# Where a tuned backbone kernel keeps its modulation blocks, and what its first transfers wait for

## The chip, the cores and the metric

One NeuronCore of a Trainium2 chip runs the whole program; the other cores are idle. The metric is the device time of one execution in microseconds, the median over several executions. The engines are named as in the profile: PE is TensorE (matmuls), PEld its weight loads, DVE is VectorE, ACT is ScalarE, POOL is GpSimd and SP is SyncE, whose queue issues nearly all DMAs here.

## The reference

Two layers of a backbone with 1024 features work on 512 latent tokens and 256 context tokens, which share the weights. Each layer has six modulation vectors for the latent tokens and six for the context tokens, made from two conditioning vectors by one large weight matrix per layer:

```python
silu_c, silu_cc = silu(c), silu(c_ctx)
for l in range(DEPTH):
    mod_lat = split(silu_c @ ada_w[l] + ada_b[l], 6)      # ada_w[l]: 1024 x 6144
    mod_ctx = split(silu_cc @ ada_w[l] + ada_b[l], 6)
    z = modulate(x, norm1_w[l], mod[0], mod[1]) @ w_in[l]  # shift, scale
    x = x + mod[2] * merge(hgrn(z), attention(z), conv(z)) @ w_out[l]
    x = x + mod[5] * square(relu(modulate(x, norm2_w[l], mod[3], mod[4]) @ w1[l])) @ w2[l]
```

`modulate` is an RMS norm times `1 + scale` plus shift. The context tokens go through the same steps in layer 0; in layer 1 only their projections are needed, so only shift and scale of the first norm are made for them there. All is float32, with inputs scaled so that low precision would show.

So the modulation is a product of two rows (latent and context) with two matrices of 6.3 million numbers: little arithmetic and much traffic.

## The kernel before

**Large products.** Activations lie with features on partitions. Every float32 product is made of three float32r matmuls: weights and activations are split into a high part and the rest (`wh`, `wl`, `Hh`, `Hl`), and `wh*Hh`, `wh*Hl`, `wl*Hh` are summed in PSUM (`fm`, L224; `tm_in`, L247, gives tokens on partitions). Weights come as **slabs** of 128 x 1024 numbers (512 KB) in a fixed plan of 304. For each slab SP issues a DMA into one of three buffers of the tag `raw` (`dma_slab`, L179), ACT makes `wh` by a copy (L205), DVE makes `wl` by a subtraction (L206). `next_w` (L209) hands out slab n, has slab n+1 split and slabs up to n+3 fetched. PE spends 24 matmuls of 512 columns on a slab for the latent tokens and 24 of 256 columns for the context tokens.

**Modulation, streamed.** `ada_stream` (L352) is a generator: `next_w` calls it once for most slabs, and each call is a step. For each piece (a block of 128 x 1024 numbers of `ada_w`) a step issues the DMA into a buffer of the same tag `raw` (L361, L363), in four strips of 256 columns, that is rows of 1 KB. One step later DVE multiplies the block by the conditioning columns and accumulates (`ada`, L376; L385 and L387): eight operations of 128 x 256 when both token kinds are needed, four when only the latent row is. After every second block follow a transpose, a reduction, eight tiny matmuls (L405) and an addition of the bias (L408). Layer 0's vectors 2, 4, 3, 5 are made in this way during the convolutions and the gates of layer 0 (32 blocks), all of layer 1's during the MLP of layer 0 (48 blocks; vectors 1 and 0 first, for which both rows are needed, 16 blocks). `self.stream` is set in `mlp` (L1117) when the first four slabs of its first quarter are through.

**The MLP.** `mlp` has four quarters e = 0 to 3; each has eight slabs of w1, whose result ACT and DVE square and split (`square`, L1105: L1112 ACT, L1113 DVE, L1114 ACT, L1115 DVE), and eight slabs of w2, whose result DVE adds to x (L1027). In the last quarter of layer 0 the w2 slabs go through `last_products` (L1080), which also gathers the squares for the next norm and begins the next layer's norm.

**The start.** `consts` (L101) issues `cc`, then the eight tiles of x in turn on ACT's and SP's queue, then small constants and the identity, from which DVE makes `sel` (L121). `start` (L299) first fetches two slabs, then block 0 of `ada_w` for the first two vectors (`ada_block`, L270: two transfers of 512 KB each, with rows of 512 bytes, into a ring of six slots; PE multiplies them with 32-column matmuls, L282). `norm_sq` (L433) squares x tile by tile on ACT (L439, L442) and sums on DVE (L443); `norm_rms` (L445) sums over partitions on PE (L452), makes the inverse root in a chain of small DVE operations and a diagonal matrix from it and the identity (L458); `norm_bc` (L462) spreads it on PE (L466). `ada_block_sum` (L286) finishes a block: ACT copy (L290), PE (L292), two DVE operations (L294, L296). Then a loop over k = 0 to 7 fetches block k+3, finishes block k+2, normalizes feature tile k (`norm_apply`, L472: L481 DVE, L483 ACT, L484 DVE) and runs the 18 matmuls of the first projection on it (L338). Its second half (L263) follows.

**The order of the work.** The code is written against a framework whose planner orders each engine's instructions: it runs the program in a model of its own and takes, of what is ready, the instruction of highest priority (earlier in the code is higher; `high_priority(offset=-30)` puts the streamed blocks' DVE work 30 places later). Buffers with a tag are handed out in turn, and whoever wants one waits for its last readers. On the chip each engine, and SP's queue, then takes its instructions in this fixed order.

## Time and profile before

| what | time |
|---|---|
| median of 3 runs | 2505.33 us (2498.78 to 2507.31) |
| profiled execution | 2507.57 us |
| its span, first to last instruction | 2505.8 us |
| PE busy | 2459.6 us (98%) |
| PEld busy | 2111.3 us (84%) |
| DVE busy | 1475.4 us (59%) |
| ACT busy | 812.6 us (32%) |
| POOL busy | 28.0 us (1%) |
| granted TensorE clock, mean | 0.998 |
| read from HBM | 226.49 MB, 92 GB/s over the span |

How to read it: busy time is the union of an engine's instructions. An idle engine costs nothing unless the one that sets the end waits for it. The list of waits puts idle time down to what ended it. A row of the windows gives, for a stretch, the busy time of PE, PEld, DVE, ACT and POOL with the number of instructions, the granted clock, the busy share of the 16 DMA engines and the GB/s. A row of the timeline has start, duration, engine, line, operation, tiles (out<-in) and, in square brackets, the engine's idle time before it with what ended it. Some matmul records can be missing.

### The profile page before, as it was taken

What the parts mean: (1) busy time and instruction counts of PE and PEld (TensorE: products, weight loads), DVE (VectorE), ACT (ScalarE), POOL (GpSimd) and SP (SyncE); (2) the same over time, 40 slices, a digit from 0 to 9 for tenths busy, and PEclk for the clock granted to TensorE, in tenths of its full rate; (3) what the DMA queues carried; (4) which work ended last, traced back from release to release, by engine and by line L of the source; (5) the groups of instructions that cost most, each with busy time, mean ns of one, the idle gap of its engine ahead of it and who ended that gap; (6) DMA issues with size and microseconds to landing.
All of it is one profiled execution on the core that took longest, in us unless ns stands there. A gap on an engine that the chain in (4) does not pass through costs nothing.

```text
span 2505.8 us, 40660 instructions
## 1 busy us (share of the span) xinstructions
PE 2459.6 (98%) x17040; PEld 2111.3 (84%) x17040; DVE 1475.4 (59%) x2952; ACT 812.6 (32%) x1435; POOL 28.0 (1%) x52
## 2 busy tenths in 40 slices
PE   7999999999999999999999999999999999999999
PEld 6888988888888888878888888888878888888887
DVE  6477867776664666675655464787653335634433
ACT  4334365321212233121222333445442223422322
POOL 0000000000000000000000000000000000000000
PEclk9999999999999999999999999999999999999999
DMA  8111112233334212333343222111222233222322
GB/s 267 60 44 45 51 53 69 77 118 118 93 118 143 76 60 85 116 113 125 120 132 119 93 76 74 52 61 49 66 74 97 97 126 108 77 94 93 101 93 93
DMA packets 112344, 233.32 MB, mean 93 GB/s; under 512 B 8224, under 2 KB 65824, under 8 KB 112160
## 3 DMA queue, kind: packets, MB, share of 16 engines
q1 hardware_dynamic: 111584, 229.14, 28.1%
q8 instruction: 134, 2.20, 0.4%
q10 hardware_dynamic: 576, 1.57, 0.2%
q14 instruction: 50, 0.41, 0.1%
HBM read 226.49 MB, written 4.19 MB: 92 GB/s over the span
## 4 chain that ended last, share of the span: by engine, by line
PE 86%; DVE 7%; DMA 5%; ACT 2%; issue 1%; SPq 0%; DVEq 0%; ACTq 0%
PE pl L239 55%; PE pc L239 15%; PE tp L263 4%; DMA ada<-in_ada_w 4%; PE pc L263 2%; DVE adac L387 2%; DVE wl L206 1%; PE av L853 1%; PE ho L645 1%; PE sc L888 1%; PE kvp L621 1%; PE ptp L934 1%; PE lv L551 1%; DVE S L590 1%; PE tp L338 1%
## 5 line engine op out<-in xcount | busy, mean ns | idle before, releaser
L205 ACT ACTIVATE wh<-raw 128x1024 fp32r<-128x1024 f32 x297 | 314.5, 1059 | 849.7 <-PE pl L239 379.2
L239 PE MATMUL pl<-Hh,wh 128*128 128x512 f32 (+1 forms) x1488 | 586.5, 394 | 0.5 <-DVE S L1002 0.5
L239 PE MATMUL pl<-Hh,wl 128*128 128x512 f32 (+1 forms) x1488 | 581.4, 391 | 3.9 <-DVE wl L206 3.9
L239 PE MATMUL pl<-Hl,wh 128*128 128x512 f32 (+1 forms) x1488 | 581.1, 391 | 0.0
L206 DVE TENSOR_TENSOR wl<-raw,wh 128x1024 fp32r<-128x1024 f32 x297 | 363.2, 1223 | 318.5 <-ACT wh L205 313.7
L239 PE MATMUL pl<-S,wh 128*128 128x512 f32 x1392 | 436.4, 395 | 2.9 <-ACT S L1114 2.8
L239 PEld LDWEIGHTS pl<-Hh,wl 128*128 128x128 f32 x1488 | 279.7, 188 | 67.8 <-DVE wl L206 7.0
L239 PEld LDWEIGHTS pl<-Hh,wh 128*128 128x128 f32 x1488 | 279.7, 188 | 57.0 <-issue 0.8
L239 PEld LDWEIGHTS pl<-Hl,wh 128*128 128x128 f32 x1488 | 279.8, 188 | 55.1 <-issue 0.5
L239 PEld LDWEIGHTS pl<-S,wh 128*128 128x128 f32 x1392 | 258.3, 188 | 57.8 <-ACT S L1114 3.2
L239 PE MATMUL pl<-S,wl 128*128 128x512 f32 x696 | 273.8, 393 | 0.0
L387 DVE SCALAR_TENSOR_TENSOR adac<-ada,sc,adac 128x256 f32<-128x256 f32 x448 | 196.4, 481 | 119.4 <-DMA ada<-in_ada_w 116.6
L239 PE MATMUL pc<-Hh,wh 128*128 128x256 f32 x872 | 244.2, 280 | 0.8 <-ACT wh L205 0.6
L239 PE MATMUL pc<-Hh,wl 128*128 128x256 f32 x872 | 244.2, 280 | 0.2 <-DVE wl L206 0.2
L239 PE MATMUL pc<-Hl,wh 128*128 128x256 f32 x872 | 244.2, 280 | 0.0
L239 PEld LDWEIGHTS pc<-Hh,wh 128*128 128x128 f32 x872 | 164.5, 189 | 5.8 <-ACT wh L205 0.8
L239 PEld LDWEIGHTS pc<-Hl,wh 128*128 128x128 f32 x872 | 164.6, 189 | 4.4 <-DVE Hl L484 0.2
L1027 DVE SCALAR_TENSOR_TENSOR S<-pl,mod,S 128x512 f32<-128x512 f32 (+1 forms) x80 | 59.2, 740 | 180.2 <-PE pl L239 180.1
L239 PEld LDWEIGHTS pc<-Hh,wl 128*128 128x128 f32 x872 | 164.3, 188 | 1.0 <-issue 0.4
L239 PEld LDWEIGHTS pl<-S,wl 128*128 128x128 f32 x696 | 131.0, 188 | 30.4
L239 PE MATMUL pc<-S,wh 128*128 128x256 f32 x688 | 127.1, 285 | 0.0
L239 PEld LDWEIGHTS pc<-S,wh 128*128 128x128 f32 x688 | 111.5, 192 | 4.4
(269 smaller groups left out, 3131.7 us busy)
## 6 DMA issues: line engine op xcount, KB each, us to landing
raw<-in_w SPq DMA_DIRECT2D x304, 512.0 KB, 3.3
ada<-in_ada_w SPq DMA_DIRECT2D x80, 512.0 KB, 4.1
S<-in_ada_w SPq DMA_DIRECT2D x16, 512.0 KB, 7.3
B<-in_bias SPq DMA_DIRECT2D x16, 448.0 KB, 4.0
S<-in_xT SPq DMA_DIRECT2D x12, 384.0 KB, 6.0
xs<-S SPq DMA_DIRECT2D x8, 256.0 KB, 2.0
S<-xs SPq DMA_DIRECT2D x8, 256.0 KB, 4.6
out<-S SPq DMA_DIRECT2D x8, 256.0 KB, 2.0
```

Source lines behind the costliest of these rows:

```text
L205: self.nc.scalar.activation(hi, r, AF.Copy)
L206: self.nc.vector.tensor_tensor(lo, r, hi, op=ALU.subtract)
L239: nc.tensor.matmul(p, lhsT=W[:, s], rhs=X[:, t0:t0 + n], start=k == 0 and i == 0, stop=k == nk - 1 and i == 2)
L263: nc.tensor.matmul(o[t], lhsT=X[:, t * 128:t * 128 + 128], rhs=W[:, k4 * 256:k4 * 256 + 256], start=piece == 0 and k4 == 0 and i == 0, sto ...
L338: nc.tensor.matmul(o[t], lhsT=X[:, t * 128:t * 128 + 128], rhs=W[:, c], start=k == 0 and i == 0, stop=k == 7 and i == 2)
L387: nc.vector.scalar_tensor_tensor(out=acc[:, row, :], in0=w, scalar=s, in1=acc[:, row, :], op0=ALU.mult, op1=ALU.add)
L551: nc.tensor.matmul(p[32 * i:32 * i + 32, c * 32:c * 32 + 32], lhsT=lhs(o), rhs=rhs(o), start=True, stop=True, tile_position=(0, 32 * i))
L590: nc.vector.tensor_tensor(qv, qv, tv, op=ALU.mult)
L621: nc.tensor.matmul(kvp[:, i * P:(i + 1) * P], lhsT=kt[:, slots[qd, c]], rhs=vh(c), start=True, stop=True)
L645: nc.tensor.matmul(po[:, i * P:(i + 1) * P], lhsT=lh, rhs=rh, start=n == 0, stop=n == len(mms) - 1)
L853: nc.tensor.matmul(po[64 * pr:64 * pr + 64, o:o + m], lhsT=nv[:, t * 256 + d0:t * 256 + d0 + 64], rhs=pts[pr][:, pc:pc + m], start=n == 0, ...
L1027: nc.vector.scalar_tensor_tensor(out=x, in0=p[:, :n], scalar=self.mod[l][:, m, j, r:r + 1], in1=x, op0=ALU.mult, op1=ALU.add)
```

## The change

Six edits:

1. The streamed blocks get buffers of their own, three of the tag `adaw`, in place of those of `raw`.
2. A block is used two steps after its DMA is issued instead of one, and its sum is finished one step later too; the generator has `len(todo) + 4` steps instead of 3 more.
3. Both kinds of modulation blocks lie in DRAM as they are wanted in SBUF: `ada1` for the start, `ada2` for the stream. A transfer has 128 rows of 4 KB, in place of rows of 512 bytes (start) or 1 KB (stream). The bytes are the same.
4. In the w1 slabs of the quarters e = 0 and e = 1 of the MLP only odd slabs make a step of the stream.
5. The identity is issued right after `cc`, ahead of x; `sel` is made after the squares of x in the code. The first two slabs are issued behind block 1 of the start instead of ahead of block 0, so their splits move behind the sums of the norm too.
6. The diagonal matrix of the start is made in two operations, 256 columns for the context tokens first, then 512.

Beside that, the memory set aside for DMA descriptors made by software is cut to 1024 (no DMA here uses it).

```diff
 consts:
         nc.sync.dma_start(out=cc, in_=self.a["cc"])
+        self.ident = self.cst("ident", [P, P])
         self.X = (11, 12, 13, 2)
...
         self.nw = self.cst("nw", [P, 2, DEPTH, 8])
-        self.ident = self.cst("ident", [P, P])
-        self.sel = sb.tile([P, 32], F32, name="sel")
-        nc.vector.tensor_reduce(out=self.sel, in_=self.ident[:, :].rearrange("p (g i) -> p i g", g=4), op=ALU.add,
-                                axis=mybir.AxisListType.X)
 ada_block:
-            self.new(ring[0])
-            r = self.S[ring[0]][:, 0:1024].rearrange("p (k f) -> p k f", k=8)
-            ring.append(ring.pop(0))
-            f0 = m * D + j * P
-            nc.sync.dma_start(out=r, in_=self.a["ada_w"][0, :, f0:f0 + P].rearrange("(k p) f -> p k f", p=P))
+            slot = ring.pop(0)
+            ring.append(slot)
+            self.new(slot)
+            r = self.S[slot][:, 0:1024].rearrange("p (k f) -> p k f", k=8)
+            nc.sync.dma_start(out=self.S[slot][:, 0:1024], in_=self.a["ada1"][j, 1 - m])
 start:
-        self.dma_slab()
-        self.dma_slab()
         ring = [0, 1, 8, 9, 10, 6]
         mp = {0: self.ada_block(0, ring)}
         self.norm_begin()
         for j in range(8):
             self.norm_sq(j, 0, T)
-        dg = self.norm_rms(0, T)
+        self.sel = self.sb.tile([P, 32], F32, name="sel")
+        nc.vector.tensor_reduce(out=self.sel, in_=self.ident[:, :].rearrange("p (g i) -> p i g", g=4), op=ALU.add,
+                                axis=mybir.AxisListType.X)
+        dg = self.norm_rms(0, T, ((512, 256), (0, 512)))
         mp[1] = self.ada_block(1, ring)
+        self.dma_slab()
+        self.dma_slab()
         self.ada_block_sum(0, mp[0])
 ada_stream:
-        for i in range(len(todo) + 3):
-            if i > 2 and todo[i - 3][2] == 1:
-                self.ada_sum(l, *todo[i - 3][:2], ahead.pop(i - 3))
+        for i in range(len(todo) + 4):
+            if i > 3 and todo[i - 4][2] == 1:
+                self.ada_sum(l, *todo[i - 4][:2], ahead.pop(i - 4))
             if i < len(todo):
                 m, c, kg = todo[i]
-                r = self.raw(f"ada{l}_{m}_{c}_{kg}")
-                f0 = m * D + c * 256
-                self.nc.sync.dma_start(
-                    out=r[:, :].rearrange("p (k f) -> p k f", k=4),
-                    in_=self.a["ada_w"][l, kg * 512:(kg + 1) * 512, f0:f0 + 256].rearrange("(k p) f -> p k f", p=P))
+                r = self.sb.tile([P, 1024], F32, tag="adaw", bufs=3, name=f"ada{l}_{m}_{c}_{kg}")
+                self.nc.sync.dma_start(out=r, in_=self.a["ada2"][l, m, c, kg])
                 ahead[i] = r
-            if 0 < i <= len(todo):
-                m, c, kg = todo[i - 1]
+            if 1 < i <= len(todo) + 1:
+                m, c, kg = todo[i - 2]
                 with self.tc.high_priority(offset=-30):
-                    ahead[i - 1] = self.ada(l, m, kg, ahead.pop(i - 1))
+                    ahead[i - 2] = self.ada(l, m, kg, ahead.pop(i - 2))
             yield
 norm_rms:
-        nc.vector.tensor_tensor(dg.rearrange("p (t q) -> p t q", q=P), self.ident[:, :].unsqueeze(1).broadcast_to([P, nt, P]),
-                                y.unsqueeze(2).broadcast_to([P, nt, P]), op=ALU.mult)
+        for p0, pn in parts or ((0, n),):
+            d = dg[:, p0:p0 + pn].rearrange("p (t q) -> p t q", q=P)
+            nb = [P, pn // P, P]
+            nc.vector.tensor_tensor(d, self.ident[:, :].unsqueeze(1).broadcast_to(nb),
+                                    y[:, p0 // P:(p0 + pn) // P].unsqueeze(2).broadcast_to(nb), op=ALU.mult)
 mlp:
             for f in range(f0, 8):
-                self.square(ff, f, self.fm(self.next_w("mlp_w1", l), *X))
+                self.square(ff, f, self.fm(self.next_w("mlp_w1", l, e > 1 or f % 2 == 1), *X))
 _host:
-    a["ada_w"] = g["ada_w"]
+    a["ada1"] = np.stack([g["ada_w"][0][:, m * D:(m + 1) * D].reshape(8, P, 8, P).transpose(2, 1, 0, 3).reshape(8, P, D)
+                          for m in (1, 0)], 1)
+    a["ada2"] = g["ada_w"].reshape(DEPTH, 2, 4, P, 6, 4, 256).transpose(0, 4, 5, 1, 3, 2, 6).reshape(DEPTH, 6, 4, 2, P, D)
 kernel:
-    nc = _bacc.Bacc("TRN2", target_bir_lowering=False, num_devices=1)
+    nc = _bacc.Bacc("TRN2", target_bir_lowering=False, num_devices=1, dynamic_dma_scratch_size=1024)
```

## The prediction

> **What bounds the kernel now.** I read the page's busy times and its chain first, then the table of waits, then windows cut at the stages, and last the timeline of two places.

> ```profile
> span 2505.8 us, 40660 instructions
> PE 2459.6 (98%) x17040; PEld 2111.3 (84%) x17040; DVE 1475.4 (59%) x2952; ACT 812.6 (32%) x1435; POOL 28.0 (1%) x52
> PE 86%; DVE 7%; DMA 5%; ACT 2%; issue 1%; SPq 0%; DVEq 0%; ACTq 0%
> ```

> TensorE sets the time: 2459.6 of 2505.8 us, so 46.2 us are idle in all. The change touches no big matmul; it can only win idle PE time and time in which PE runs slowly. So the question is where PE stands still because of modulation blocks. The waits:

> ```profile
> DVE adac L387 <- DMA ada<-in_ada_w: 116.6, 37, 5.7
> DVE adac L385 <- DMA ada<-in_ada_w: 84.5, 37, 5.2
> PE adap L282 <- DMA S<-in_ada_w: 16.7, 2, 16.1
> ```

> The columns are total us, times, longest. DVE waits 201 us for streamed blocks, but that is no loss by itself: PE pays only where something behind the waiting DVE instruction is needed at once. The MLP of layer 0 shows where. I cut it at the first matmul that reads Hh (w1 begins) or S (w2 begins); the rows below are w2 of e=0, then w1 and w2 of e=1, w1 and w2 of e=2, w1 and w2 of e=3:

> ```profile
> 991.59:1060.05 68.46, 68.46 (x424) 59.98 (x416) 47.34 (x106) 9.17 (x11) 0.00 (x0) 1.00 0.35 108
> 1060.05:1133.66 73.61, 69.74 (x424) 58.76 (x416) 51.56 (x110) 19.84 (x35) 0.00 (x0) 1.00 0.36 115
> 1133.66:1208.46 74.80, 71.93 (x424) 62.10 (x416) 40.31 (x77) 10.78 (x14) 0.00 (x0) 0.95 0.41 127
> 1208.46:1275.75 67.29, 67.29 (x425) 58.78 (x417) 40.68 (x82) 21.54 (x37) 0.00 (x0) 1.00 0.40 126
> 1275.75:1344.14 68.39, 68.39 (x425) 59.80 (x417) 39.29 (x75) 9.89 (x12) 0.00 (x0) 1.00 0.38 124
> 1344.14:1411.16 67.02, 67.02 (x417) 58.66 (x410) 34.97 (x65) 22.51 (x38) 0.00 (x0) 1.00 0.32 103
> 1411.16:1479.73 68.57, 68.49 (x394) 59.82 (x393) 35.47 (x69) 20.04 (x34) 0.56 (x2) 1.00 0.30 103
> ```

> The stages of e=1 do the matmuls of e=2 and take 73.61 + 74.80 = 148.41 us against 67.29 + 68.39 = 135.68: **12.7 us too much**, of which PE idles 3.87 + 2.87 us. How one stall arises, in order of time:

> ```profile
> 1132.60 1.22 DVE L206 TENSOR_TENSOR wl<-raw,wh 128x1024 fp32r<-128x1024 f32 x1
> 1133.85 0.38 SPq L363 DMA_DIRECT2D ada<-in_ada_w  x1
> 1139.78 0.49 DVE L387 SCALAR_TENSOR_TENSOR adac<-ada,sc,adac 128x256 f32<-128x256 f32 x1 [4.71 <-DMA ada<-in_ada_w]
> 1140.18 0.69 DVE L1113 TENSOR_TENSOR B<-B 128x512 f32<-128x512 f32 x1
> 1140.90 0.63 ACT L1114 ACTIVATE S<-B 128x512 fp32r<-128x512 f32 x1 [5.81 <-DVE B L1113]
> 1141.59 1.65 PE L239 MATMUL pl<-S,wh 128*128 128x512 f32 x2 [2.81 <-ACT S L1114]
> ```

> Slabs and blocks share the three raw buffers. The block's DMA is issued when the slab split ends (1132.60 + 1.22) and its data is wanted straight away, 5.9 us later DVE goes on, and the square of the MLP behind it in DVE's queue, ACT's copy and PE follow. A window right behind that gap (its third column from the end is the granted clock):

> ```profile
> 1141.01:1147.83 6.82, 6.18 (x24) 5.49 (x25) 5.19 (x11) 2.16 (x4) 0.00 (x0) 0.50 0.48 149
> ```

> After 2.81 us of idle PE the clock is 0.50 for 6.82 us, which is another 3.4 us.

> **Part 1, the stream (layer 0's second one).** New: the blocks have three buffers of their own, are issued two steps ahead of use, and in w1 of e=0 and e=1 only every second step takes one. A step is one slab, about 68.4/8 = 8.5 us, so a block now has some 17 us to land.

> ```profile
> raw<-in_w SPq DMA_DIRECT2D x304, 512.0 KB, 3.3
> ada<-in_ada_w SPq DMA_DIRECT2D x80, 512.0 KB, 4.1
> ```

> These are issues by line, KB each, and median us to landing. Landing takes 4.1 us in the median (5.9 above): hidden under two slabs; if that cover were gone, the 4 to 5 us wait is back at each step. DVE's load in w1 of e=1 becomes that of e=2: there, eight blocks with one row each; here, four with two rows, 32 operations either way. So I take 67.29 us for w1 of e=1. For its w2 I take e=0's 68.46, a stage of two-row blocks without idle PE. Gain 148.41 - 135.75 = **12.7 us**. Bounds: 6 (half of the stalls stay, because DVE's order and not the DMA holds the squares) to 13.

> [...]

> The first stream runs in the convolutions and gates of layer 0:

> ```profile
> 500.00:550.00 50.00, 50.00 (x304) 43.71 (x303) 40.35 (x91) 8.46 (x13) 0.00 (x0) 1.00 0.38 122
> ```

> The planner also orders everything else anew; stages with PE full can't gain by that and can lose, which the rivals hold. PE has no idle here, with DVE busy 40.35 of 50 us: nothing to win, and I put nothing.

> New waits: SP now holds block i until DVE has finished block i-3; the next slabs' DMAs are queued behind. Block i-3 is worked on one step earlier, and a slab issued in step n is split in step n+2, so about 17 - 3.3 = 13 us of delay are free.

> Moved steps: six steps are skipped in w1 of e=0 and e=1 and the pipeline is one longer (52 instead of 51), so the blocks now run until the sixth w2 step of e=3. That stage has DVE 35.47 of 68.57 us; four one-row blocks of about 4 x 0.49 us and their transposes fit. Behind it comes the norm, whose DVE work PE waits for: I put 0.5 us against the change (0 to 2).

> **Part 2, the start.** Its timeline:

> ```profile
> 6.35 0.43 SPq L98 DMA_DIRECT2D c_ident<-in_ident  x1
> 8.06 0.80 SPq L185 DMA_DIRECT2D raw<-in_w  x2
> 10.03 28.91 SPq L279 DMA_DIRECT2D S<-in_ada_w  x16
> 6.86 0.96 DVE L443 TENSOR_TENSOR S<-S,S 128x768 f32<-128x768 f32 x1 [2.48 <-ACT S L442]
> 11.73 0.37 DVE L121 TENSOR_REDUCE sel<-c_ident 128x32 f32<-128x128 f32 x1 [3.91 <-DMA c_ident<-in_ident]
> 18.07 1.22 DVE L206 TENSOR_TENSOR wl<-raw,wh 128x1024 fp32r<-128x1024 f32 x1
> 19.21 0.95 DVE L443 TENSOR_TENSOR S<-S,S 128x768 f32<-128x768 f32 x1
> 16.07 1.08 PE L282 MATMUL adap<-S,sc 128*32 128x128 f32 x16 [16.07 <-DMA S<-in_ada_w]
> 17.79 1.08 PE L282 MATMUL adap<-S,sc 128*32 128x128 f32 x16 [0.63 <-DMA S<-in_ada_w]
> 20.25 2.70 PE L452 MATMUL nms<-ones,S 128*128 128x2 f32 x12
> 25.40 0.96 DVE L458 TENSOR_TENSOR S<-c_ident,nst 128x768 f32<-128x768 f32 x1
> ```

> And windows of it; the last column is GB/s, the first busy time PE's:

> ```profile
> 6.00:8.00 2.00, 0.00 (x0) 0.00 (x0) 0.96 (x1) 1.56 (x2) 0.00 (x0) 1.00 1.04 415
> 20.00:22.00 2.00, 2.00 (x11) 2.00 (x11) 0.55 (x3) 0.00 (x0) 0.00 (x0) 1.00 1.17 290
> 16.07:31.16 15.09, 13.45 (x128) 10.85 (x129) 9.13 (x26) 3.81 (x8) 0.00 (x0) 1.00 1.18 291
> 31.16:58.82 27.66, 27.66 (x331) 24.28 (x330) 22.96 (x59) 13.42 (x26) 0.00 (x0) 1.00 0.78 236
> ```

> Transfers: xT, in rows of 3 KB, ran at 415 GB/s (its 3.1 MB are through at about 10.3 us); the blocks, in rows of 512 bytes, at 290. In transfer order (4 KB rows) I give them xT's rate. A half block of 0.524 MB then takes 1.26 us instead of 1.81. Two slabs (1.05 MB, 2.5 us) no longer stand ahead. First half block: 16.07 - 2.5 - 0.55 = 13.0; second: 17.79 - 2.5 - 1.1 = 14.2. The rate pays only until TensorE is the limit.

> [...]

> DVE: the reduction of the identity held the sums for 3.91 + 0.37 us and the two slab splits (one is shown) for 2 x 1.22; without them seven adds of 0.95 from 6.86 end at about 13.8 instead of 20.16. ident ahead of x delays x by one issue, 0.4 us. The norm's matmuls go behind block 0: 14.2 + 1.1 = 15.3, end 18 instead of 22.95. The dependent DVE chain (2.4 us) and the first, smaller part of the diagonal (one more instruction, about 0.2) end at 20.8 instead of 26.36.

> That is 5.5 us on the norm's chain, but not all of it counts. PE was busy 13.45 of 15.09 us before the first big matmul (31.16), with work that stays, and 27.66 of 27.66 us from there to the next stage (58.82). Starting at 13.0 instead of 16.07, the first stretch ends at 26.5 to 28.1 (its idle time gone or kept): 3.1 to 4.7 us earlier. The slab splits, 2.44 us of DVE, now fall between 19 us (their landing: 10.3, four half blocks, two slabs, and the 1.3 us that 16.07 lies behind 10.3 + 2.5 + 1.8) and 26; they fit. I take **4 us**. Bounds: -1 (a split that stands in DVE's queue ahead of the norm's chain waits for its slab until 19.2) to 7 (the norm chain's whole 5.5 and PE's 1.64 us of idle before the loop).

> **Sum.** 12.7 - 0.5 + 4.0 = 16.2 us. The profiled execution took 2507.57 us (span 2505.8 and 1.8 around it), the median of the three runs is 2505.33, 2.2 less. 2507.6 - 16.2 = 2491.4 and 2505.3 - 16.2 = 2489.1: I say **2490**.

> **Rivals.** *Only the stream pays* (17%): the start's order turns out so that the splits or PE's own work take it back; 2505.3 - 12.2 = 2493. For it: PE is nearly full from 16.07 on. Against: its first operand comes 3 us sooner.

> *The stalls stay* (18%): the two-row blocks, placed ahead of the squares in DVE's queue, and not the DMA, hold PE. Then e=1 wins at most 3 us and the start 4 at most: about 2499 to 2504. For it: DVE is busiest just there, 51.56 of 73.61. Against: w2 of e=0 has 47.34 of 68.46 with no idle PE, and the longest stall ends with a DMA.

> *Slower* (7%): SP's queue. In the first stream, where DVE has 81% of its time taken, a block is finished more than a step late, SP stands at the next block's buffer and the slab behind it lands late. The price per step is that of today's stalls, 12.7/16 = 0.8 us; over that stream's 36 steps 29 us, so 2505.3 + 29 - 16 = 2518. It decides once a block runs about 13 us late, more than a step and a half; at 81% load DVE has room, so I hold it unlikely.

> **How the numbers follow.** Forecast 58%, 2490. A change under 0.3% (7.5 us) can't be told from none here. Forecast and "only the stream" are faster: 75%. "The stalls stay" is within 0.3%: 18%. Slower: 7%. The three runs spread from 2498.78 to 2507.31, and that spread goes into the range: from 2482 (the lowest run less 16.2) to 2504 (the highest less 3, the stalls staying). It leaves out the slower case and a little on either side.

> **What would show it.** w1 and w2 of e=1 at 67 to 69 us each with the clock at 1.00; DVE's waits for blocks down from 201 us to under 30; the slab DMAs of SP never late; blocks at the start at about 400 GB/s; the sums done near 14 us, the first big matmul before 28.5 and the next stage before 56. I am wrong if e=1 keeps its 148 us, or if a stage that had no idle PE gets some.

## The result and the profile after

The changed kernel takes **2492.79 us** in the median of five executions (2492.56 to 2494.19), the kernel before beside it 2504.32 us (2498.78 to 2507.31). The ratio is 0.9949 with a 95% interval of 0.9939 to 0.996: faster by about 11.5 us. (The 2505.33 us that the prediction starts from is the median of the first three of the five executions before.) The profiled execution took 2493.18 us (span 2491.4), that of before 2507.57 (2505.8).

From the page of the changed kernel, its busy times, its chain, and its DMA issues (KB each, median us to landing):

```profile
span 2491.4 us, 40672 instructions
...
PE 2456.6 (99%) x17040; PEld 2109.3 (85%) x17040; DVE 1485.6 (60%) x2953; ACT 816.1 (33%) x1435; POOL 27.5 (1%) x52
...
PE 93%; DVE 3%; ACT 2%; issue 1%; DMA 1%; SPq 0%; DVEq 0%; ACTq 0%
...
raw<-in_w SPq DMA_DIRECT2D x304, 512.0 KB, 3.2
ada<-in_ada SPq DMA_DIRECT2D x80, 512.0 KB, 3.2
```

PE's busy time is 3 us less, though it has the same 17040 matmuls; its idle time went from 46.2 to 34.8 us. DVE has left most of the chain (7% to 3%), DMA too (5% to 1%). DVE's waits for blocks, which were 201 us in 74 times (columns: total us, times, longest):

```profile
DVE adac L384 <- DMA ada<-in_ada: 9.7, 13, 1.6
DVE adac L382 <- DMA ada<-in_ada: 1.0, 1, 1.0
DVE mod L405 <- PE adap L402: 72.0, 20, 6.3
```

The third row is a new wait: DVE now stands 72 us for the tiny matmuls of finished blocks, against 6.3 us before. Nearly all of it lies between 503 and 809 us, and PE is busy for all of the 310 us from 500 to 810, so it costs nothing there.

And windows at the same cuts of the MLP: w1 and w2 of e=1, w2 of e=3, and the stretch behind it, in which the next layer's norm begins; the last row is that stretch in the kernel before:

```profile
1055.81:1122.63 66.82, 66.82 (x403) 58.52 (x401) 40.80 (x81) 23.15 (x38) 0.00 (x0) 1.00 0.28 95
1122.63:1190.93 68.30, 68.30 (x419) 59.13 (x417) 40.53 (x78) 9.17 (x10) 0.00 (x0) 1.00 0.41 141
...
1394.08:1463.60 69.52, 69.45 (x418) 60.27 (x417) 36.05 (x73) 20.15 (x34) 0.56 (x2) 1.00 0.30 101
1463.60:1505.47 41.87, 38.86 (x305) 37.45 (x304) 22.22 (x42) 12.07 (x18) 0.00 (x0) 0.96 0.17 57
...
1479.73:1520.67 40.94, 36.75 (x306) 35.20 (x304) 22.23 (x42) 12.07 (x18) 0.00 (x0) 1.00 0.17 58
```

The pair of e=1 fell from 148.41 to 135.12 us, with PE full and the clock at 1.00: 13.29 us. w2 of e=3 took 0.95 us more. The last stretch took 0.93 more; its clock is 0.96 here, and was 1.00 before.

The start, in order of its engines (timeline; the row of ACTq is the issue of four DMAs by ACT):

```profile
0.73 3.89 ACTq L109 DMA_DIRECT2D S<-in_xT  x4
4.65 1.28 ACT L114 ACT_TABLE_LOAD   x1 [4.65 <-DMA S<-in_xT]
8.27 1.58 ACT L439 ACTIVATE S<-S 128x768 f32<-128x768 f32 x2 [1.38 <-DMA S<-in_xT]
9.14 0.96 DVE L440 TENSOR_TENSOR S<-S,S 128x768 f32<-128x768 f32 x1 [2.77 <-ACT S L439]
15.52 0.96 DVE L440 TENSOR_TENSOR S<-S,S 128x768 f32<-128x768 f32 x1
13.68 2.23 PE L279 MATMUL adap<-S,sc 128*32 128x128 f32 x32 [13.68 <-DMA S<-in_ada]
17.29 2.70 PE L449 MATMUL nms<-ones,S 128*128 128x2 f32 x12
23.47 0.16 DVE L291 TENSOR_TENSOR mod<-adap,c_adab 128x4 f32<-128x4 f32 x1 [1.47 <-PE adap L289]
24.00 1.03 DVE L458 TENSOR_TENSOR S<-c_ident,nst 128x256 f32<-128x256 f32 x2
28.29 0.50 PE L338 MATMUL tp<-wh,Hh 128*128 128x256 f32 x2
```

The second square waits for the second tile of x, which lands at 8.24 us by the trace, 5.96 before; so the first addition of the norm's sums begins at 9.14 us, 6.86 before.

Two windows of it, from the first block to the first big matmul, and from there to the next stage:

```profile
13.68:28.29 14.61, 13.20 (x128) 10.56 (x129) 9.28 (x27) 4.93 (x9) 0.00 (x0) 1.00 0.98 391
28.29:55.78 27.49, 27.49 (x329) 24.10 (x329) 23.31 (x60) 13.51 (x26) 0.00 (x0) 1.00 0.62 215
```

The first big matmul begins 2.87 us earlier, the next stage 3.04 us earlier (55.78 after 58.82). In profiles that makes 13.29 + 3.04 - 0.95 - 0.93 = 14.45, and the two spans differ by 14.4; the other stretches cancel (1.2 us won between 60 us and e=1, 0.45 lost in e=2 and e=3, 0.8 behind). The medians differ by 11.5; what is known of the other 3 us is told below.

One thing was not expected. The two rows are the DMA issues and the first operations of the streamed blocks (times: first and last start):

```profile
L362 SPq DMA_DIRECT2D ada<-in_ada x80: 327/328/1152, 56.9 to 1356.7; - x80
L382 DVE TENSOR_SCALAR adac<-ada,sc x64: 340/346/355, 62.2 to 1371.4; 128x256 f32<-128x256 f32 x64
```

The first block is issued at 56.9 us; before, the first was issued at 413.5. With buffers of their own the blocks no longer wait behind slabs for a place, and the planner pulls them ahead of the program's steps as far as three buffers reach: nine of the first stream between 56.9 and 88.1, nine of the second between 740 and 816 (before: the second stream began at 949.4). A step of the generator says when a block may be asked for at the latest; it does not say when it runs.

### The profile page after: what moved, and what is told of

Its sections match the earlier page's. It is cut to its first block, busy times and chain, and to the rows that moved or that the text cites. A ratio compares the mean times of both kernels' runs of the same rounds, so it can differ in the third digit from the quotient of the medians.

```text
span 2491.4 us, 40672 instructions
## 1 busy us (share of the span) xinstructions
PE 2456.6 (99%) x17040; PEld 2109.3 (85%) x17040; DVE 1485.6 (60%) x2953; ACT 816.1 (33%) x1435; POOL 27.5 (1%) x52
## 4 chain that ended last, share of the span: by engine, by line
PE 93%; DVE 3%; ACT 2%; issue 1%; DMA 1%; SPq 0%; DVEq 0%; ACTq 0%
PE pl L236 60%; PE pc L236 18%; PE tp L260 4%; PE pc L260 2%; PE sc L888 1%; PE av L853 1%; PE ho L645 1%; PE ptp L934 1%; PE kvp L621 1%; PE lv L551 1%; DVE S L590 1%; ACT wh L202 1%; PE tp L338 1%; DVE wl L203 0%; PE lv L579 0%
## 5 line engine op out<-in xcount | busy, mean ns | idle before, releaser
L202 ACT ACTIVATE wh<-raw 128x1024 fp32r<-128x1024 f32 x297 | 314.9, 1060 | 872.6 <-PE pc L236 409.4
L384 DVE SCALAR_TENSOR_TENSOR adac<-ada,sc,adac 128x256 f32<-128x256 f32 x448 | 201.8, 479 | 15.7 <-DMA ada<-in_ada 9.7
## 6 DMA issues: line engine op xcount, KB each, us to landing
raw<-in_w SPq DMA_DIRECT2D x304, 512.0 KB, 3.2
ada<-in_ada SPq DMA_DIRECT2D x80, 512.0 KB, 3.2
S<-in_ada SPq DMA_DIRECT2D x16, 512.0 KB, 5.4
```

The source lines that it names most:

```text
L202: self.nc.scalar.activation(hi, r, AF.Copy)
L384: nc.vector.scalar_tensor_tensor(out=acc[:, row, :], in0=w, scalar=s, in1=acc[:, row, :], op0=ALU.mult, op1=ALU.add)
```

## The experiments

The first four kernels each make one part of the change on the kernel before (2506.91 us on their chip, 19 executions). Their expectations name three theories of what holds e=1. A: slabs and blocks wait for each other through the shared buffers. B: there are too many two-row blocks per slab in w1. C: the blocks land too slowly.

**Own buffers alone.**

```diff
-                r = self.raw(f"ada{l}_{m}_{c}_{kg}")
+                r = self.sb.tile([P, 1024], F32, tag="adaw", bufs=3, name=f"ada{l}_{m}_{c}_{kg}")
```

> The kernel before with one edit of the change: the streamed blocks get three buffers of their own. Rows of 1 KB, one step ahead, every step of w1 and the old start stay. Measured are w1 and w2 of e=1 in layer 0's MLP: 148.4 us together before, 135.1 after the whole change. Theory A (the loop: slabs and blocks wait for each other through the shared buffers): own buffers alone bring the pair to 135 to 138 us, DVE's waits for blocks fall from 201 us to under 50, and the time is 2491 to 2495. Theory B (too many two-row blocks per slab in w1): the pair stays above 143 and the time above 2499. Theory C (the blocks land too slowly): as B.

2495.46 us, ratio 0.9958 (0.9943 to 0.9972). Windows, w1 and w2 of e=1:

```profile
1059.57:1127.67 68.10, 68.10 (x425) 59.55 (x417) 47.43 (x95) 23.15 (x39) 0.00 (x0) 1.00 0.44 139
1127.67:1196.61 68.94, 68.94 (x424) 59.82 (x416) 37.08 (x70) 9.18 (x11) 0.00 (x0) 1.00 0.39 123
```

No idle PE, 137.04 us: 11.4 of the pair's 13.3 us with one edit, blocks in rows of 1 KB, used one step after their issue, at every slab. The pair is where A put it, the time half a microsecond over A's range. (This kernel and the one with six shared buffers also have the change's smaller memory for descriptors; the lighter w1 alone, without it, gains nearly as much.)

**The lighter w1 alone.**

```diff
-                self.square(ff, f, self.fm(self.next_w("mlp_w1", l), *X))
+                self.square(ff, f, self.fm(self.next_w("mlp_w1", l, e > 1 or f % 2 == 1), *X))
```

> The kernel before with one edit: in w1 of e=0 and e=1 only odd slabs make a step of the stream. Buffers are shared as before. Theory A: the loop is still there in each step that has a block, so the pair w1 and w2 of e=1 keeps part of its 13 us, 140 to 146, and the time is 2496 to 2502. Theory B: the pair falls to 137 or less and the time to 2491 to 2494. Theory C: as A.

2496.54 us, ratio 0.9962 (0.9948 to 0.9977). The same two windows, and DVE's waits for blocks in the whole span:

```profile
1059.72:1127.49 67.77, 67.59 (x411) 58.66 (x409) 44.88 (x91) 22.56 (x39) 0.00 (x0) 1.00 0.34 109
1127.49:1196.17 68.68, 68.68 (x424) 59.74 (x416) 40.40 (x82) 9.17 (x11) 0.00 (x0) 1.00 0.38 122
```

```profile
DVE adac L387 <- DMA ada<-in_ada_w: 115.6, 37, 5.8
DVE adac L385 <- DMA ada<-in_ada_w: 93.3, 36, 5.6
```

This run settles more than any other. The pair is where B put it, the time in A's range. DVE still waits 209 us for blocks, as long as before, and yet the pair is down to 136.45 us. Over the whole program those waits cost nothing by themselves. In w1 of e=1 of the kernel before, PE's own waits were (total us, times, longest; window 1060 to 1147 us):

```profile
PE pl L239 <- DVE wl L206: 3.9, 6, 1.1
PE pl L239 <- ACT S L1114: 2.8, 1, 2.8
```

Six splits of slabs and one square came late. What holds DVE in this stage is the wait for blocks and the operations on them (0.34 to 0.49 us each), and both can be counted in w1 of e=1 of each kernel:

| kernel | operations on blocks, us (number) | waits for blocks, us | idle PE, us |
|---|---|---|---|
| before | 23.45 (55) | 18.6 | 3.87 |
| start's order alone | 23.44 (55) | 18.3 | 3.81 |
| rows of 4 KB alone | 22.35 (53) | 16.7 | 2.06 |
| lighter w1 alone | 16.27 (39) | 12.9 | 0.18 |
| six shared buffers | 18.19 (42) | 9.0 | 0 |
| changed, block at every slab | 20.16 (45) | 0 | 0 |
| own buffers alone | 17.91 (40) | 0 | 0 |
| changed | 12.93 (31) | 0 | 0 |

PE stands still where blocks take 39 us or more of DVE, and next to not at all at 29 us or less. Own buffers do not only end the wait: as in the changed kernel, nine blocks of this stream are then fetched and worked on long before, so that this stage gets one two-row block and eight one-row ones instead of five two-row blocks and parts of four others, and a quarter of the operations leaves it. No kernel here has the old number of operations without the waits, so which of the two counts for how much is not shown. A alone would have kept this pair at 140 or more, B alone that of own buffers above 143: either cure is enough, and together they give 1.3 to 1.9 us more than one.

**Rows of 4 KB alone** (both kinds of blocks; the buffers and the order are those of before).

```diff
-                self.nc.sync.dma_start(
-                    out=r[:, :].rearrange("p (k f) -> p k f", k=4),
-                    in_=self.a["ada_w"][l, kg * 512:(kg + 1) * 512, f0:f0 + 256].rearrange("(k p) f -> p k f", p=P))
+                self.nc.sync.dma_start(out=r, in_=self.a["ada2"][l, m, c, kg])
```

> The kernel before with one edit: both kinds of blocks lie in DRAM in the order in which they are wanted, rows of 4 KB instead of 512 bytes and 1 KB. Theory A: a block lands about 1 us sooner, the loop stays, the pair of e=1 is 143 to 147 and the time 2499 to 2503. Theory C: the pair falls to 138 or less, 2494 or less. The start: the sums of the norm (done at 20.2 us) and the two slabs ahead of block 0 hold it as before, so the first big matmul stays at 30.0 to 31.2 and the next stage (58.8 before, 55.8 after) begins at 57.5 to 58.8; if the rate of the transfers is what the start waits for, at 56.5 or less.

2500.49 us (2498.17 to 2505.26), ratio 0.9975 (0.9966 to 0.9984).

```profile
1060.63:1131.51 70.88, 68.82 (x425) 58.92 (x417) 50.62 (x108) 19.92 (x36) 0.00 (x0) 1.00 0.38 121
1131.51:1203.62 72.11, 69.72 (x424) 59.76 (x417) 40.17 (x76) 10.71 (x14) 0.00 (x0) 1.00 0.40 130
```

Two thirds of the stalls are left (4.45 us of idle PE of 6.74). So theory C (138 or less) does not hold. The pair is 5.4 us shorter than in before's profile; 2.2 of it are PE's busy time in w2 (69.72 against 71.93), where the clock stayed at 1.00 here. The gain of 6.4 us by the medians isn't found in these stages, and the next stage at the start even begins at 60.48, 1.7 us later than before and outside both expectations; its executions spread over 7 us, and where the rest lies stays open.

**The start's order alone** (edits 5 and 6; blocks in rows of 512 bytes; the diff is theirs, above).

> The kernel before with the two edits of the start: identity ahead of x, first slabs behind block 1, reduction of the identity behind the squares, diagonal in two parts. Rows of 512 bytes stay, and the stream is as before. If the order is what the start gained by: the first big matmul at 28.3 to 29.5 us (31.2 before, 28.3 after) and the next stage at 55.8 to 57 (58.8 before, 55.8 after). If the rate of the transfers made it: 30 to 31 and 57.5 to 58.8. The pair of e=1 stays at 146 to 150 by either, and the time is 2501 to 2503.

2504.97 us, ratio 0.9998 (0.9988 to 1.0007): 1.9 us by the medians, no change by the interval, and above the 2501 to 2503 expected. The first big matmul is at 29.43 and the next stage begins at 57.28, 1.54 us earlier; the second lies between the two expectations. Its MLP is that of before, and shows the same stages in another execution:

```profile
1059.49:1132.85 73.36, 69.55 (x425) 58.69 (x417) 51.55 (x110) 19.86 (x35) 0.00 (x0) 1.00 0.36 115
1132.85:1204.79 71.94, 69.38 (x424) 59.19 (x416) 39.64 (x76) 10.77 (x14) 0.00 (x0) 1.00 0.42 132
```

The longest stall is there again, from the timeline:

```profile
1140.04 0.50 PE L236 MATMUL pl<-S,wh 128*128 128x512 f32 x1 [2.04 <-ACT S L1117]
```

It is 2.04 us long, not 2.81, and the clock stays at 1.00: w2 takes 71.94, not 74.80, with 2.55 us less of busy PE. So the half clock behind the stall does not belong to this stage in every execution; why it was spared here is not shown.

The next four ran on another chip, beside 2506.34 us for the kernel before (15 executions). Now the rivals were: own buffers win because blocks no longer share a queue of buffers with slabs, or because there are more buffers; the lighter w1 adds something to them, or not; ACT's late begin holds the start, or not.

**Six shared buffers** on the kernel before, the same memory as three and three.

```diff
-        return self.sb.tile([P, 1024], F32, tag="raw", bufs=3, name=name)
+        return self.sb.tile([P, 1024], F32, tag="raw", bufs=6, name=name)
```

> The kernel before with six shared raw buffers in place of three: as much memory as own buffers take, but slabs and blocks are still handed out from one ring. If what the change removed is that blocks and slabs share (theory A), the order of the ring still ties a block's DMA to the split of a slab, and w1 and w2 of e=1 stay above 143 us (148.4 before, 136.9 with own buffers alone). If it is the depth alone, three more buffers do the same: 135 to 138, and a time of 2494 to 2496.

2503.56 us, ratio 0.9988 (0.9979 to 0.9997). Its windows: w1 and w2 of e=1, and 394 to 440 us.

```profile
1064.18:1132.28 68.10, 68.10 (x425) 59.55 (x417) 45.32 (x95) 22.21 (x37) 0.00 (x0) 1.00 0.39 124
1132.28:1201.22 68.94, 68.94 (x424) 59.82 (x416) 38.39 (x74) 9.88 (x12) 0.00 (x0) 1.00 0.38 123
...
394.00:440.00 46.00, 42.54 (x306) 33.93 (x304) 42.20 (x117) 25.74 (x63) 0.62 (x2) 1.00 0.29 93
```

Depth alone heals e=1 as fully as own buffers, but the time is not the 2494 to 2496 that went with it. Here the first stream's blocks are pulled ahead too, to 391.5 us, where DVE has no room: it is busy 42.20 of 46 us (35.56 before), and PE gets a new wait, from the list of 394 to 571 us:

```profile
PE vtr L779 <- DVE S L750: 2.4, 1, 2.4
```

The stretch from 394 to w_out takes 3.1 us more in this profile. It wins 6.3 us in the span but 2.8 in the medians; its profiled execution is the fastest of its ten, and where the others lose the rest isn't shown.

**The changed kernel with a block at every slab of w1** (edit 4 undone).

```diff
-                self.square(ff, f, self.fm(self.next_w("mlp_w1", l, e > 1 or f % 2 == 1), *X))
+                self.square(ff, f, self.fm(self.next_w("mlp_w1", l), *X))
```

> The changed kernel with one edit undone: every w1 slab of e=0 and e=1 makes a step again. Own buffers alone and pacing alone each took nearly all of e=1's loss away, so they should be two cures of one illness: the pair of e=1 stays at 135 to 138 us without pacing. The blocks end some steps sooner, so w2 of e=3 (69.5 us after the change, 68.6 before) should go back to 68.4 to 68.8 if the late blocks cost it the 0.9. Time 2491.5 to 2493.5. If the pacing is needed beside the buffers: the pair at 139 or more and 2495 or more.

2494.74 us, ratio 0.9951 (0.9938 to 0.9963), that of the changed kernel on other chips within 0.1%, though not the 2491.5 to 2493.5 expected. w1 and w2 of e=1, then w2 of e=3:

```profile
1057.94:1125.75 67.81, 67.81 (x418) 59.18 (x417) 49.07 (x100) 23.15 (x38) 0.00 (x0) 1.00 0.44 142
1125.75:1194.05 68.30, 68.30 (x419) 59.15 (x418) 37.43 (x70) 9.17 (x10) 0.00 (x0) 1.00 0.38 123
...
1397.20:1465.61 68.41, 68.34 (x394) 59.62 (x393) 35.47 (x69) 20.05 (x34) 0.56 (x2) 1.00 0.31 103
```

w1 of e=1 takes 0.99 us more than in the changed kernel and w2 of e=3 1.11 less. No stall is behind it, PE is full in all of them. Grouped by line, the changed kernel's PE has in its w2 of e=3 one group that this kernel has not:

```profile
L402 PE MATMUL adap<-adar,sel 128*32 128x2 f32 x24 | 0.7, 182 | 0.0
```

These are the tiny matmuls of three finished blocks. Beside own buffers edit 4 carries PE's work from one full stage to another, and no run here shows that it is worth anything.

**All tiles of x on SP's queue** in the changed kernel, so that ACT issues no DMA.

```diff
-            (nc.sync if j % 2 else nc.scalar).dma_start(out=self.xb(j), in_=self.a["xT"][j])
+            nc.sync.dma_start(out=self.xb(j), in_=self.a["xT"][j])
```

> The changed kernel with all eight tiles of x issued on SP's queue instead of in turn on ACT's and SP's. In the changed kernel ACT's fourth issue stood in its queue until 4.6 us, and the table load and all squares behind it (first square 6.07 us, 4.26 before). If that is why the sums end at 16.5 and not at the 13.8 that was forecast, the table load goes back to 2.6 to 3, the sums end at 14 to 15, the norm's matmuls begin at 15.9 to 16.3 instead of 17.3, and the next stage (55.8) at 54.3 to 55. If x's landing sets the squares: no change within 0.4 us.

2494.84 us, ratio 0.9951 (0.9937 to 0.9964).

```profile
0.73 1.28 ACT L114 ACT_TABLE_LOAD   x1 [0.73 <-PEq L1221]
...
14.15 0.96 DVE L440 TENSOR_TENSOR S<-S,S 128x768 f32<-128x768 f32 x1
...
14.36 1.08 PE L279 MATMUL adap<-S,sc 128*32 128x128 f32 x16 [14.36 <-DMA S<-in_ada]
...
15.37 2.72 PE L449 MATMUL nms<-ones,S 128*128 128x2 f32 x12
...
30.73 0.48 PE L338 MATMUL tp<-wh,Hh 128*128 128x256 f32 x2
```

The table load comes at once and the norm's sums end at 15.11, 1.4 us earlier. But it need not be ACT's begin that did this: on one queue the second tile of x is also there sooner: the second square, which waits for it, begins at 6.50 us instead of 8.27, and the first addition follows at 7.37. The last run below parts the two. The next stage begins at 56.58, not at the 54.3 to 55 expected but between the changed kernel's own two (55.78, and 56.75 in its second profile): PE did more of the blocks' matmuls ahead of the first big one instead of behind it.

**The identity behind x again** in the changed kernel.

```diff
-        self.ident = self.cst("ident", [P, P])
         self.X = (11, 12, 13, 2)
...
         self.nw = self.cst("nw", [P, 2, DEPTH, 8])
+        self.ident = self.cst("ident", [P, P])
```

> The changed kernel with the identity issued behind x and the small constants again, the rest of the start new. If the identity's place ahead of x is what pushes ACT's fourth issue back, the first square goes back to 4.0 to 4.4 and the sums end at 14 to 15, unless the reduction of the identity stands in DVE's queue ahead of them; then the old wait for it (3.9 us) is back and the sums end at 17 to 18. Next stage at 54.3 to 55.2 in the first case, 56.5 to 58 in the second.

2494.8 us, ratio 0.9952 (0.9939 to 0.9966). The next stage begins at 57.42; the sums end at 18.31, since the reduction of the identity holds DVE again. The first square is back at 4.03 and the first addition at 6.49, but that reduction then takes the gain away, as the second case of the expectation has it. By the time it can't be told from the changed kernel.

The last three ran on one chip, beside 2505.83 us (nine executions).

**The changed kernel once more.**

> The changed kernel itself, beside the two below on one chip. Both theories: the same as in its first runs, 11 to 13 us under the kernel before, first big matmul 28 to 29 us, next stage 55.5 to 56.5 us; its spread over executions smaller than that of the kernel before.

2494.40 us (2493.48 to 2494.78), ratio 0.9953 (0.994 to 0.9967): 11.4 us. First big matmul 29.29, next stage 56.75, so the start alone differs by 1 us between two executions of one kernel. The pair of e=1 is 66.81 + 68.31, the same within 0.01. The stretch behind the MLP went by at a clock of 1.00:

```profile
1465.69:1506.62 40.93, 36.74 (x306) 35.19 (x304) 22.23 (x42) 12.08 (x18) 0.00 (x0) 1.00 0.17 59
```

0.94 us less than in the first profile, where the clock was 0.96: that kernel's loss there is one of some executions as well. Slow matmuls alone do not make it: with a block at every slab those of `pc<-wh,Hl` take 305 ns in the mean in this stretch, 314 in the first profile and 287 before, and it takes 40.94.

**The start as before** in the changed kernel (edits 5 and 6 undone; the 4 KB rows stay).

```diff
-        self.ident = self.cst("ident", [P, P])
         self.X = (11, 12, 13, 2)
...
+        self.dma_slab()
+        self.dma_slab()
         ring = [0, 1, 8, 9, 10, 6]
...
-        dg = self.norm_rms(0, T, ((512, 256), (0, 512)))
+        dg = self.norm_rms(0, T)
```

> The changed kernel with edits 5 and 6 undone (identity, sel, first two slabs and the diagonal as before); the 4 KB rows of the start stay. Theory A (the new order of the start is worth 2 to 3 us of time on the path, as the profile of the changed kernel has it): first big matmul near 31, next stage near 59, time 2 to 3 us above the changed kernel on the same chip. Theory B (what the start gives is within what one execution differs from the next, and PE's work at the start sets the time): next stage within 1 us of the changed kernel, time within 1 us.

2496.28 us (2495.75 to 2498.06), 1.9 us over the changed kernel on the same chip; the lowest of its five lies above the highest there. In its profile the sums end at 19.75, the first big matmul is at 30.75 and the next stage at 58.68, 1.93 us after that of the run beside it. So edits 5 and 6 are worth 1.9 us on this chip, and all that is left of the change 2505.83 - 2496.28 = 9.6 us.

**Block 0 ahead of the second half of x** in the changed kernel, with three tiles of x on ACT's queue: an attempt to beat it.

```diff
-            (nc.sync if j % 2 else nc.scalar).dma_start(out=self.xb(j), in_=self.a["xT"][j])
+            (nc.scalar if j in (0, 2, 4) else nc.sync).dma_start(out=self.xb(j), in_=self.a["xT"][j])
+            if j == 3:
+                for h in range(2):
+                    self.new(h)
+                    nc.sync.dma_start(out=self.S[h][:, 0:1024], in_=self.a["ada1"][0, h])
```

> The changed kernel with both halves of the start's block 0 issued after the fourth tile of x instead of behind the eighth, and ACT issuing three tiles of x instead of four. If the start is bound by PE's own work from its first operand on (42.1 us from 13.68 to 55.78): block 0's 2.2 us of matmuls run before 13 us, the next stage starts 2 to 3 us earlier, at 53 to 54, and the time falls by as much. If the norm's chain (sums 16.5, sums over partitions 17.3 to 20, diagonal 24, first big matmul 28.3) binds: first big matmul within 0.5 us of the changed kernel's and the next stage at most 1 us earlier. If x is delayed by the two transfers: sums over 17.5 and the next stage later than 56.

2493.80 us (2492.52 to 2494.78) beside 2494.40: the ranges overlap.

```profile
8.45 1.58 ACT L445 ACTIVATE S<-S 128x768 f32<-128x768 f32 x2 [3.64 <-DMA S<-in_xT]
...
10.92 2.27 PE L285 MATMUL adap<-S,sc 128*32 128x128 f32 x32 [10.92 <-DMA S<-in_ada]
...
17.55 2.72 PE L455 MATMUL nms<-ones,S 128*128 128x2 f32 x12 [2.83 <-DVE S L446]
...
28.49 0.61 PE L344 MATMUL tp<-wh,Hh 128*128 128x256 f32 x2
```

PE begins 2.8 us earlier and then stands still 2.83 us for the norm's sums; the next stage begins at 56.05, between the changed kernel's two. The run also tells what holds the sums. ACT's table load is at 2.14 us and its first square at 3.97, as early as before the change, yet the second square waits until 8.45 for the second tile of x, and the sums end at 17.49, later than the changed kernel's 16.48 and 16.81. So it is the landing of that tile, and not ACT's late begin. With x on SP's queue the norm's chain was moved ahead, here PE's work on the blocks (with the chain 0.7 to 1 us later), and neither moved the end. That fits two chains of about equal length; no run moved one and kept the other as it was.

## Why the prediction was right, and where it was not

The time, 2492.79 against 2490, is inside the range, and faster was the likeliest case. Of the 15.3 us that were forecast from the median 11.5 came; the stages gained 14.4 of 16.2 in the profiles. By its steps:

- **Which stage pays**: right. The pair of e=1 gave 13.29 us in the profile against 12.7 forecast, PE full and the clock at 1.00 in both stages, DVE's waits for blocks at 10.7 us. All seven profiles with the changed buffers and lead, with a block at every slab or not, have the pair between 135.1 and 136.2 us.
- **What holds PE there**: half right. The chain shown (late block, square behind it in DVE's queue, ACT, PE) was one stall of 2.81 us; six others, 3.9 us in all, were late splits of slabs. That buffers, lead and the lighter w1 were priced as one edit hid that each of two edits is enough, and that the lighter w1 shows no gain beside the buffers.
- **The half clock as a gain of every execution**: wrong as a step, and by the stages the larger part of the miss. The prediction took 3.4 us of the 12.7 from a clock row of one execution and subtracted the sum from the median. The same stage in another execution (the start's order alone) had a stall of 2.04 us and went by at full clock: 71.94 against 74.80 in w2, 2.55 of it PE's busy time. Against that execution the pair's gain is 145.30 - 135.12 = 10.2 us, and all edits but 5 and 6 measure 9.6 by times, where 12.2 were forecast (own buffers alone measured 11.4 on their chip, with an interval of 7 to 14). The profiled execution of before lies 3.25 us above its five runs' median, so the profiles differ by 14.4 and the medians by 11.5. That the clock makes this difference is not shown: there is one profile of that kernel. Of its 43 executions beside the experiments 21 have a mean clock of 0.998 and 22 of 0.999 or 1.000, and their mean times, 2506.9 and 2506.2, lie only 0.6 us apart. Without the 3.4 us the sum would have been 9.3 for the stream, and the 9.6 by times are nearer to it than to 12.7. Within the spans of the two profiles, before and after, the trace lists four drops to 0.50, three of 3.41 us and one of 6.83: the long one is that of e=1, behind the gap of 2.81 us. What brought each drop is not shown.
- **The start, 4 us**: right in direction, too large: 3.04 in the first profile, 2.07 in the second, 1.9 by times. Step by step: the first block at 13.68 (13.0 forecast; 14.21 in the second profile), the second half after it by 1.1 us. Half blocks of the start that follow each other land 1.2 to 1.3 us apart (13.54, 14.78, 16.05, 17.32), as forecast, against 1.80 or 1.81 before (15.94, 17.74, 19.55, 21.36). With the start's order alone, which keeps the rows of 512 bytes, PE begins on the second half 1.41 us after the first (14.41 and 15.82). So in these runs the rows of 4 KB landed faster than those of 512 bytes. The sums were to end at 13.8 and ended at 16.48. What failed is "ident ahead of x delays x by one issue, 0.4 us": the second tile of x was issued 0.47 us later (1.64 instead of 1.17) but landed 2.28 us later (8.24 instead of 5.96), and the first addition moved by the same 2.28. The rest is the seven additions, which follow each other every 1.06 us and not every 0.95. x was also not through at 10.3 us in the kernel before: its eighth tile landed at 11.17. The diagonal began at 24.00, where its first part was to be done at 20.8: 2 us of that are the late sums; and in DVE's queue the bias of block 1 (L291, shown above) stood ahead of the chain's last steps and waited 1.47 us for PE. Of the signs named for the start, the first big matmul before 28.5 and the next stage before 56 came true in one profile (28.29, 55.78) and not in the other (29.29, 56.75).
- **w2 of e=3, 0.5 us against the change**: 0.95 measured, and for another reason than "blocks now run until the sixth w2 step": the last block is worked on at 1375 us, before that stage begins. What moved in are tiny matmuls, and as much left w1 of e=1, so that the net is near nothing.
- **The steps as a clock** (17 us to land, issue two steps ahead): wrong as a picture, since the planner runs ahead of the steps. For the sum it was harmless: w1 of e=1 has 31 operations on blocks where 32 were forecast.
- **Rivals.** "The stalls stay" fell, in the stage it named. "Only the stream pays" (2493) has the right number; but the start pays 1.9 us and the stream less than it said. "Slower" by SP's queue did not come: slabs land in 3.2 us in the median, 3.3 before, and in both stages of e=1 PE waits for no split.
- **Nothing to win in the first stream, nothing lost by the new order**: the rows do not contradict it; the change of order is large (blocks at 57 us), and the stages of the MLP in which PE was full kept their times within 1 us. The run with six shared buffers shows that this was not sure.

## What to carry to other kernels

A long list of waits on an engine that isn't the bound says little: 209 us of DVE's waits stayed and the gain came all the same; look for the few waits of the engine that sets the end, and ask which one instruction each time came late. Take a clock drop that one profile shows as the property of that execution until a second shows it at the same place, and make the sum without it when the base is a median. When one transfer is put ahead of others, ask where the one that the first operation waits for will land, not only by how much it is issued later: here 0.47 us became 2.28. Where two chains seem to end together, as the norm and PE's work do at this start, expect little from shortening one of them.

## What the runs showed of the hardware

**Slow weight loads under a clock of 1.00.** At the start the weight loads of 128 x 128 take 333 ns and later 188, while the profile's clock column says 1.00 throughout. Of the changed kernel, grouped by form, at 17 to 20 us and at 36 to 40:

```profile
L449 PEld LDWEIGHTS nms<-ones,S 128*128 128x128 f32 x12 | 2.7, 333 | 0.0
...
L338 PEld LDWEIGHTS tp<-wh,Hl 128*128 128x128 f32 x4 | 0.8, 188 | 0.0
```

That 1.00 is no measurement there. The trace's list of granted clocks has its first entry, 1.00, at 27.25 us here and at 31.68 in the kernel before, and the windows give 1.00 for the time ahead of it too (13.68 to 28.29 us here, 16.07 to 31.16 before). The weight loads become fast within 1 us of that entry in both traces: 333 ns at 26 to 27 us and 188 at 27 to 28 here, 334 at 29 to 30 us and 192 at 32 to 33 before. So they are slow until 13.6 us after the first matmul here and 15.6 before, though here PE was busy 13.20 of 14.61 us ahead of the first big matmul, mostly with small matmuls. With 4 KB rows alone sixteen 32-column matmuls still take 1.08 us at 32.89 us, where before they take 0.64 at 32.49, and the loop behind the first big matmul takes 29.6 us against 27.7. The entry comes 2.7 us after the twelve 128-column matmuls that spread the norm begin here, 4.4 before. What sets its moment was not tried.
